# Two transformer blocks on one core: products moved between engines, keys repeated by transfers, and work moved around a loop over heads

## The chip, the cores and the metric

One core of a Trainium2 chip runs the whole program; the time is the device time of one execution in microseconds. TensorE (PE) multiplies, VectorE (DVE), ScalarE (ACT) and GpSimd (POOL) do the element-wise work, and SyncE (SP) issues most transfers between the device's memory and the core. Each engine has one stream of instructions, which it takes in order; an instruction that waits holds up the ones behind it on its engine.

## The reference

512 tokens of width 1024 go through two blocks in float32:

```
first block:  x += rms(mixer(rms(x)));  x += rms(memory attention(rms(x)));  x += rms(swiglu(rms(x)))
second block, two layers:
  q, k, v, z_attn, z_ssm, xbc, dt = split(x @ w_in)
  attn = sliding_window_attention(q, k, v, sinks) * silu(z_attn)      16 heads of 64, 4 key heads
  xbc  = silu(causal_conv4(xbc));  xs, B, C = split(xbc)              12 groups of 128 channels
  y    = chunked_state_space(xs, dt, a, B, C) + xs * d_skip           16 heads of 64, chunks of 128
  ssm  = gated_rmsnorm(y, z_ssm)                                      2 groups of 512 channels
  x    = layer_norm(alpha * x + concat(attn, ssm) @ w_out)
```

The memory attention has 4 heads of 128 over 256 memory rows. Its softmax and that of the windows are over keys on the free axis, with queries on partitions.

## The kernel before

Activations lie transposed, channels on 128 partitions and the 512 tokens on the free axis. Every float32 product is made from three products of rounded halves: a value is split into `hi` (rounded by ACT, L107, L129, L132) and `lo` (the rest, by DVE, L108, L130, L133), and `mm3` (L140 to L152) multiplies hi by hi, hi by lo and lo by hi. A *projection* (`proj`, L185) is one weight tile of 1024 columns against the eight tiles of `h`: 24 matmuls of 512 columns. `weights` (L100) gets such a tile: a transfer of 512 KB on SP into `wraw`, then `whi` on ACT and `wlo` on DVE, with three buffers of each. `held` (L111) splits the weights into activation tiles of 512 columns instead (tags G and R, 34 tiles each), which live as long as they are used.

The order on ACT, DVE, POOL and PE is laid out by a planner that takes, at each moment of its own reckoning, the ready instruction that stands first in the program. SP is exempt (`manual_schedule`, L1375): its transfers stay in the program's order.

Memory (`memory`, L721) works on halves A and B of the tokens: queries of A, logits and softmax of A (L743 to L764), queries of B with the values of A in between, then the output product `out(j, c)` (L791) with four tiles of `w_o_mem`, of which three come through `weights`. `post_norm` (L308) gives each half a chain: a norm over the sum of squares (`rstd`, L200), then eight steps that update x, store it to `xd` (L788) and prepare the next stage's `h` (L263 to L266). The swiglu stage begins with four weight tiles at once (L845, L846) and runs `units_by_k` (L160) over half A, then half B.

Each layer of `hybrid` (L885) makes four gates, the convolutions of B and C (`conv`, L901), convolutions 0 to 4 of xs, and then a loop over eight pairs of heads: `decay(j+1)` (two matmuls L1041, relu and exp on ACT L1045 to L1048, a product L1049, on POOL for the even head), `heads(j)` (16 matmuls L1061, 6 matmuls L1067 and DVE's L1069 to L1071), the gate (L1098) and a sum of squares. In between the loop makes one projection for each of j = 0 to 6: convolutions 5 to 7, then four gates. Iteration 6 norms the first group (`gated_norm(0)`, L1073). After the loop come two key projections, each split by halves of 64 partitions and repeated on the other 64 by POOL (L1114), then the values (96 matmuls of 256 columns, L1127 to L1129), `gated_norm(1)`, and attention:

```
q = queries(0)
for t in range(17):
    j, e_ = divmod(t, 2)
    nxt = scores(t, q) if t < 16 else None
    if t: pts[t - 1] = transposed(prs)
```

`scores` (L1136) makes the logits (L1154, L1155), DVE's bias and maximum (L1160), exp (L1164) and the products with the reciprocal sum (L1169: four parts, two on DVE and two on POOL); `transposed` turns the parts on PE (L1183).

Of the kernel before, what the change touches and what calls it, by code (L numbers as in the profile page):

```python
# [8 lines left out]
F32 = mybir.dt.float32  # L9
F32R = mybir.dt.float32r  # L10
AF = mybir.ActivationFunctionType
ALU = mybir.AluOpType

P = 128
S = 512
# [46 lines left out]
class Kern:  # L62
# [4 lines left out]
    def __init__(self, ctx, tc, aps):  # L67
        self.ctx, self.tc, self.nc, self.a = ctx, tc, tc.nc, aps
        pool = lambda name, **kw: ctx.enter_context(tc.tile_pool(name=name, **kw))
        self.cp = pool("const", bufs=1)  # L70
        self.wp = pool("wts", bufs=3)
        self.rp = pool("acts", bufs=1)
        self.sp = pool("small", bufs=1)
        self.pp = pool("psum", bufs=1, space=bass.MemoryType.PSUM)
        self.dp = pool("scratch", bufs=1, space=bass.MemoryType.DRAM)
        self.n = 0
        self.head = None


    def nm(self, s):  # L80
# [19 lines left out]
    def weights(self, src, n=1024):  # L100

        nc = self.nc
        raw = self.wp.tile([P, 1024], F32, tag="wraw", bufs=3, name=self.nm("wraw"))
        nc.sync.dma_start(raw[:, :n], src)
        hi = self.wp.tile([P, 1024], F32R, tag="whi", bufs=3, name=self.nm("whi"))
        lo = self.wp.tile([P, 1024], F32R, tag="wlo", bufs=3, name=self.nm("wlo"))
        nc.scalar.copy(hi[:, :n], raw[:, :n])  # L107
        nc.vector.tensor_tensor(lo[:, :n], raw[:, :n], hi[:, :n].bitcast(F32), ALU.subtract)  # L108
        return hi, lo

    def held(self, src, tag, n=1024):  # L111
# [612 lines left out]
    def memory(self):  # L724


        nc, a = self.nc, self.a
        h, rs = self.h, self.rs
# [14 lines left out]
        def logits(hd, c):  # L743

            kh, kl = mk[hd]
            qh, ql = q[hd]
            bank = self.ps("lg")
            for i in range(2):
                qq = slice(c.start + i * P, c.start + i * P + P)
                for n, (l, r) in enumerate(((qh, kh), (qh, kl), (ql, kh))):  # L750
                    nc.tensor.matmul(bank[:, 256 * i : 256 * i + 256], l[:, qq], r[:, :256], start=n == 0, stop=n == 2)
            st = self.s("st4", (P, 20), 2)
            mx, nm, sm, rc = (st[:, 2 * i : 2 * i + 2] for i in range(4))
            pr = self.f("R")
            nc.vector.tensor_reduce(mx, bank.rearrange("p (b k) -> p b k", b=2), mybir.AxisListType.X, ALU.max)
            r = rs[:, c.start // P : c.start // P + 2]
            nc.vector.scalar_tensor_tensor(nm, mx, -1.0, r, ALU.mult, ALU.mult)
            parts = [pr[:, 256 * i : 256 * i + 256] for i in range(2)]
            for i, p in enumerate(parts):
                nc.scalar.activation(p, bank[:, 256 * i : 256 * i + 256], AF.Exp, bias=nm[:, i : i + 1], scale=r[:, i : i + 1], accum_out=sm[:, i : i + 1])  # L760
            nc.vector.reciprocal(rc, sm)
            for i, p in enumerate(parts):
                (nc.vector if i else nc.gpsimd).tensor_scalar(p, p, rc[:, i : i + 1], 1.0, ALU.mult, ALU.mult)
            return parts  # L764

        def values(hd, c, prs):
# [18 lines left out]

        def each(k, c, x):
            scale(k, c, x)
            nc.scalar.dma_start(self.xd[k][:, c], x)  # L788

        def out(j, c):  # L790
            o = self.ps()[:, :256]  # L791
# [8 lines left out]
            nc.sync.dma_start(kv[i].bitcast(F32), self.spill[i])  # L800
        wo = [self.held(a["w_o_mem"][0], "G")]
        queries(B, lambda k: values(k // 2, A, pa[k // 2]) if k % 2 else None)
        wo += [self.weights(a["w_o_mem"][1]), self.weights(a["w_o_mem"][2])]
        for j in range(8):
            if j == 4:
                wo.append(self.weights(a["w_o_mem"][3]))
            out(j, A)
            if j < 4:
                pb.append(logits(j, B))
        for j in range(4):  # L810
            values(j, B, pb[j])
            if j == 0:
                self.head = chain(A)
                self.begin()
# [7 lines left out]
    def ffn(self):  # L822
# [19 lines left out]
        full = slice(0, S)  # L842
        hid += self.pairs("R", 2)
        g = [self.f("ht") for _ in range(2)]
        first = [self.weights(z) for z in (a["w_gate"][0], a["w_up"][0], a["w_gate"][1])]  # L845
        first.append(self.held(a["w_up"][1], "R"))  # L846
        for c in self.HALVES:
            for i, pt in enumerate(self.units_by_k(first, h, c)):
                (up if i % 2 else gate)(i // 2, c, g[i // 2][:, c], pt)
# [15 lines left out]

        def src(k, c):
            t = self.s("w256", (P, 256), 9)
            nc.scalar.dma_start(t, self.xd[k][:, c])
            return t

        self.h = self.pairs("G")
# [15 lines left out]
    def hybrid(self, L):  # L887
# [25 lines left out]
        def silu(t, pz):  # L913

            self.tanh(t, pz, scale=0.5)
            nc.vector.scalar_tensor_tensor(t, t, 1.0, pz, ALU.add, ALU.mult)
# [113 lines left out]
            xs.append(conv(j, "G"))  # L1030
        xs.append(conv(4, "G"))
        tokens(0)

        def decay(j):

            ee = self.f("R")
            dfs = []
            for e_ in range(2):
                hd = 2 * j + e_
                pb = self.ps("lg")  # L1040
                nc.tensor.matmul(pb, self.sel[:, hd : hd + 1].broadcast_to([48, P]), ahl, start=True, stop=True)  # L1041
                df = self.f("R")
                for c in range(4):
                    cc = slice(c * P, (c + 1) * P)
                    nc.scalar.activation(df[:, cc], pb[:, cc], AF.Relu, bias=atok[:, c * 16 + hd : c * 16 + hd + 1], scale=-1.0)  # L1045
                rows = slice(64 * e_, 64 * e_ + 64)
                nc.scalar.activation(ee[rows, P:], pb[rows, P:], AF.Exp)
                nc.scalar.activation(df, df, AF.Exp, scale=-1.0)  # L1048
                (nc.vector if e_ else nc.gpsimd).tensor_tensor(df, df, cb[hd // 8], ALU.mult)  # L1049
                dfs.append(df)  # L1050
            return dfs, ee

# [26 lines left out]
                cat[8 + i] = self.pair(t, "R")  # L1079


        cat = [None] * 16
        accs = []
        ws = decay(0)
        for j in range(8):
            g = j // 4
            if j < 3:
                xs.append(conv(5 + j, "G"))
            elif j < 7:
                zs.append(self.f("R"))  # L1090
                silu(zs[-1], self.proj(W[25 + j], h))
            nxt = decay(j + 1) if j < 7 else None
            if j == 3:
                tokens(1)
            heads(j, *ws)
            ws = nxt
            y = xs[j]
            nc.vector.tensor_tensor(y, y, zs[j], ALU.mult)  # L1098
            if j == 6:
                gated_norm(0, accs[0])  # L1100
            if j % 4 == 0:
                accs.append(self.f("acc"))
            self.sumsq(y, accs[-1], j % 4 == 0)


        top, bot = slice(0, 64), slice(64, P)
        kt = []
        for j in range(2):
            pt = self.proj(W[j], h)
            ks = [[self.r("G") for _ in range(2)] for _ in range(2)]  # L1110
            for (kh, kl), r, o in zip(ks, (top, bot), (bot, top)):
                self.split(pt[r], kh[r], kl[r], 0.125)
                for t in (kh, kl):
                    nc.gpsimd.tensor_copy(t[o], t[r].bitcast(F32))  # L1114
            kt.append(ks)
        vs = [self.f("G") for _ in range(2)]
        pv = [self.ps("mm") for _ in range(2)]
        for c in range(2):
            wh, wl = self.weights(W[2 + c])
            for t in range(4):  # L1120
                o = pv[t // 2][:, 256 * (t % 2) : 256 * (t % 2) + 256]
                tt = slice(t * P, (t + 1) * P)
                for kk in range(4):
                    k = 4 * c + kk
                    ws = slice(256 * kk, 256 * kk + 256)
                    st = k == 0 and t % 2 == 0
                    nc.tensor.matmul(o, h[k][0][:, tt], wh[:, ws], start=st, stop=False, skip_group_check=True)  # L1127
                    nc.tensor.matmul(o, h[k][0][:, tt], wl[:, ws], start=False, stop=False, skip_group_check=True)
                    nc.tensor.matmul(o, h[k][1][:, tt], wh[:, ws], start=False, stop=k == 7, skip_group_check=True)  # L1129
        for v, pt in zip(vs, pv):  # L1130
            nc.scalar.copy(v, pt)

        gated_norm(1, accs[1])

        def scores(t, q):
# [30 lines left out]
            nc.vector.tensor_tensor(sm, sm, es, ALU.add)  # L1166
            nc.vector.reciprocal(rc, sm)  # L1167
            for b in range(4):
                (nc.gpsimd if b % 2 else nc.vector).tensor_scalar(prs[b], prs[b], rc[:, b : b + 1], 1.0, ALU.mult, ALU.mult)  # L1169
            return prs  # L1170

        def transposed(prs):
# [34 lines left out]
            return qs  # L1207


        q = queries(0)  # L1210
        gate, pts = {}, {}
        prs = None
        for t in range(17):
# [17 lines left out]
                cat[i] = self.pair(gate[i], "R", 0.5)  # L1231
            prs = nxt

        order = list(range(8, 16)) + list(range(8))
        acc, acc2, rs = self.f("acc"), self.f("acc"), self.f("rs")
        vs = [self.f("G") for _ in range(KD)]
# [186 lines left out]
```

## Time and profile before

| | us |
|---|---|
| median of 3 runs (1672.94 to 1673.29) | 1673.09 |
| profiled execution, its own time | 1672.5 |
| its span, first to last instruction | 1670.7 |
| PE busy, share of the span | 1621.6, 97% |
| DVE, ACT, POOL busy | 1115.1, 838.0, 239.2 |

The span has 24187 instructions, 9046 of them matmuls. A busy PE is not PE at its peak, since ends of matmuls are modelled; the granted clock has two levels, 2.4 GHz (written 1.00) and 1.2 GHz (0.50).

### The profile page before, as it was taken

The numbers are of one execution on the slowest core, as the hardware profiler recorded it, in microseconds if no ns is written. First come the engines' busy times: TensorE is split into PE (matmuls) and PEld (weight loads), VectorE is DVE, ScalarE is ACT, GpSimd is POOL, SyncE is SP. The second block draws the span as 40 slices with busy tenths as digits, with TensorE's granted clock in tenths as the row PEclk, the third lists the DMA queues.
The fourth block names the chain that finished last, engine by engine and source line by source line (L and its number), as shares of the span: only waits on it lengthen the run. The fifth ranks groups of instructions, "written<-read, shape, count | busy, mean of one in ns | idle before, by whom it ended". The sixth has DMA issues, their size and how long they took to land.

```text
span 1670.7 us, 24187 instructions
## 1 busy us (share of the span) xinstructions
PE 1621.6 (97%) x9046; PEld 1362.4 (82%) x9046; DVE 1115.1 (67%) x2199; ACT 838.0 (50%) x1648; POOL 239.2 (14%) x267
## 2 busy tenths in 40 slices
PE   8999999999999999999999999999999999999996
PEld 5778888889888888889988677777998867777786
DVE  6779866548885545523677888765487788866447
ACT  4443255336763233223554776664355477766424
POOL 2010113010200000000000223221230023222121
PEclk9999999999999999999999999999999999999998
DMA  6522322143143233234632122111452211212133
GB/s 223 196 96 76 119 96 76 64 151 119 62 150 104 89 101 101 87 102 129 212 93 89 38 64 89 64 64 56 141 177 82 79 38 57 96 61 65 66 103 112
DMA packets 57719, 166.50 MB, mean 100 GB/s; under 512 B 6673, under 2 KB 15841, under 8 KB 57601
## 3 DMA queue, kind: packets, MB, share of 16 engines
q1 hardware_dynamic: 49216, 155.21, 29.0%
q10 hardware_dynamic: 8384, 9.73, 1.8%
q8 instruction: 71, 1.16, 0.3%
q14 instruction: 48, 0.39, 0.1%
HBM read 158.61 MB, written 8.93 MB: 100 GB/s over the span
## 4 chain that ended last, share of the span: by engine, by line
PE 78%; DVE 11%; ACT 5%; issue 2%; POOL 2%; DMA 1%; SPq 0%; ACTq 0%; DVEq 0%; POOLq 0%
PE psmm L148 21%; PE psmm L152 21%; PE psmm L147 21%; DVE wlo L108 2%; POOL w L1169 2%; PE psmm L175 2%; PE psmm L173 2%; PE psmm L174 2%; ACT w L1164 1%; DVE w L1160 1%; DVE G L130 1%; PE pstr L1061 1%; PE pstr L1183 1%; PE pslg L561 1%; PE pslg L1020 1%
## 5 line engine op out<-in xcount | busy, mean ns | idle before, releaser
L147 PE MATMUL psmm<-G,whi 128*128 128x512 f32 (+1 forms) x1196 | 468.5, 393 | 1.3 <-ACT whi L107 1.3
L148 PE MATMUL psmm<-G,whi 128*128 128x512 f32 (+1 forms) x1196 | 464.3, 389 | 0.0
L108 DVE TENSOR_TENSOR wlo<-wraw,whi 128x1024 fp32r<-128x1024 f32 (+3 forms) x265 | 320.4, 1210 | 184.8 <-ACT whi L107 99.2
L107 ACT CAST whi<-wraw 128x1024 fp32r<-128x1024 f32 (+3 forms) x265 | 270.9, 1025 | 340.3 <-PE psmm L148 291.3
L152 PE MATMUL psmm<-G,wlo 128*128 128x512 f32 (+1 forms) x1196 | 296.3, 388 | 0.0
L148 PEld LDWEIGHTS psmm<-G,whi 128*128 128x128 f32 x1196 | 225.3, 188 | 47.2 <-issue 4.2
L147 PEld LDWEIGHTS psmm<-G,whi 128*128 128x128 f32 x1196 | 225.3, 188 | 47.2 <-issue 2.4
L152 PEld LDWEIGHTS psmm<-G,wlo 128*128 128x128 f32 x1196 | 222.7, 189 | 46.4 <-issue 1.5
L148 PE MATMUL psmm<-R,whi 128*128 128x256 f32 (+1 forms) x732 | 222.7, 326 | 0.0
L147 PE MATMUL psmm<-R,whi 128*128 128x256 f32 (+1 forms) x732 | 222.6, 326 | 0.0
L147 PEld LDWEIGHTS psmm<-R,whi 128*128 128x128 f32 x732 | 139.2, 190 | 11.8 <-issue 0.3
L148 PEld LDWEIGHTS psmm<-R,whi 128*128 128x128 f32 x732 | 139.2, 190 | 11.5
L152 PE MATMUL psmm<-R,wlo 128*128 128x256 f32 (+1 forms) x732 | 138.1, 326 | 0.0
L152 PEld LDWEIGHTS psmm<-R,wlo 128*128 128x128 f32 x732 | 112.8, 190 | 11.5
L198 POOL TENSOR_TENSOR acc<-acc,sq 128x512 f32<-128x512 f32 (+1 forms) x42 | 53.4, 1272 | 454.4 <-ACT sq L197 454.4
L1164 ACT ACTIVATE w<-w,st 128x256 f32<-128x256 f32 (+1 forms) x128 | 60.2, 471 | 33.5 <-DVE st L1162 33.2
L1169 POOL TENSOR_SCALAR w<-w,st 128x256 f32<-128x256 f32 x64 | 46.1, 730 | 134.6 <-DVE st L1167 127.0
L209 ACT ACTIVATE sq<-ht 128x512 f32<-128x512 f32 (+1 forms) x48 | 29.4, 613 | 58.5 <-DVE ht L907 29.3
L1049 POOL TENSOR_TENSOR R<-R,R 128x512 f32<-128x512 f32 x16 | 21.7, 1353 | 228.3 <-ACT R L1048 228.3
L907 DVE SCALAR_TENSOR_TENSOR ht<-psmm,cwh,ht 128x511 f32<-128x511 f32 (+2 forms) x72 | 53.5, 743 | 1.2
L837 DVE TENSOR_TENSOR sq<-psmm,G 128x512 f32<-128x512 f32 (+1 forms) x24 | 15.5, 645 | 57.3 <-PE psmm L152 57.3
L566 POOL TENSOR_TENSOR G<-G,G 128x384 f32<-128x384 f32 (+2 forms) x24 | 28.9, 1217 | 162.1 <-DMA G<-ts 93.4
(348 smaller groups left out, 2701.8 us busy)
## 6 DMA issues: line engine op xcount, KB each, us to landing
wraw<-w_in SPq DMA_DIRECT2D x112, 512.0 KB, 3.4
wraw<-w_out SPq DMA_DIRECT2D x56, 512.0 KB, 3.8
wraw<-w_down SPq DMA_DIRECT2D x24, 512.0 KB, 3.5
wraw<-w_gate SPq DMA_DIRECT2D x22, 512.0 KB, 3.3
wraw<-w_up SPq DMA_DIRECT2D x22, 512.0 KB, 3.3
wraw<-w_down SPq DMA_DIRECT2D x12, 384.0 KB, 3.2
wraw<-w_proj_attn SPq DMA_DIRECT2D x8, 512.0 KB, 3.4
ts<-t SPq DMA_DIRECT2D x4, 640.0 KB, 7.0
```

The lines of the kernel that those rows point to most:

```text
L107: nc.scalar.copy(hi[:, :n], raw[:, :n])
L108: nc.vector.tensor_tensor(lo[:, :n], raw[:, :n], hi[:, :n].bitcast(F32), ALU.subtract)
L147: nc.tensor.matmul(out, whi[:, c], xh, start=start and k == 0, stop=False)
L148: nc.tensor.matmul(out, whi[:, c], xl, start=False, stop=False)
L152: nc.tensor.matmul(out, wlo[:, c], xh, start=False, stop=stop and k == n - 1)
L173: nc.tensor.matmul(o, whi[:, cc], xh[:, c], start=k == 0 and i % 2 == 0, stop=False, skip_group_check=True)
L174: nc.tensor.matmul(o, whi[:, cc], xl[:, c], start=False, stop=False, skip_group_check=True)
L175: nc.tensor.matmul(o, wlo[:, cc], xh[:, c], start=False, stop=k == n - 1, skip_group_check=True)
L198: (eng or nc.gpsimd).tensor_tensor(acc, acc, t, ALU.add)
L907: nc.vector.scalar_tensor_tensor(y[:, s:], pt[:, : S - s], cw(3 - s), y[:, s:], ALU.mult, ALU.add)
L1164: nc.scalar.activation(prs[b], prs[b], AF.Exp, bias=nm[:, b : b + 1], accum_out=sm[:, b : b + 1])
L1169: (nc.gpsimd if b % 2 else nc.vector).tensor_scalar(prs[b], prs[b], rc[:, b : b + 1], 1.0, ALU.mult, ALU.mult)
```

## The change

Seven edits. (1) All softmax products of memory and of the windows go to DVE. (2) Between the start of attention and its end, `lo` of a weight tile is made in two pieces of 512 columns. (3) The stores to and loads from `xd` go from ACT's queue to SP's. (4) Memory's output weights 1 to 3 are held in R tiles, all loaded before `out`, and the first three weight tiles of the swiglu stage are asked for before the values of half B. (5) Convolutions 5 and 6 stand ahead of the loop. (6) In the loop, the even head's relu goes to DVE (as a minimum with the sign turned) and its product from POOL to DVE. (7) The loop's projections are now convolution 7, four gates, the values (j = 5) and the two keys (j = 6 and 7); the keys are repeated by four transfers on SP each.

```diff
+        self.piece = 2 * S
...
-        nc.vector.tensor_tensor(lo[:, :n], raw[:, :n], hi[:, :n].bitcast(F32), ALU.subtract)
+        for o in range(0, n, self.piece):
+            c = slice(o, min(o + self.piece, n))
+            nc.vector.tensor_tensor(lo[:, c], raw[:, c], hi[:, c].bitcast(F32), ALU.subtract)
...
-                (nc.vector if i else nc.gpsimd).tensor_scalar(p, p, rc[:, i : i + 1], 1.0, ALU.mult, ALU.mult)
+                nc.vector.tensor_scalar(p, p, rc[:, i : i + 1], 1.0, ALU.mult, ALU.mult)
...
-            nc.scalar.dma_start(self.xd[k][:, c], x)
+            nc.sync.dma_start(self.xd[k][:, c], x)
...
-        wo += [self.weights(a["w_o_mem"][1]), self.weights(a["w_o_mem"][2])]
+        wo += [self.held(a["w_o_mem"][j], "R") for j in (1, 2, 3)]
         for j in range(8):
-            if j == 4:
-                wo.append(self.weights(a["w_o_mem"][3]))
             out(j, A)
             if j < 4:
                 pb.append(logits(j, B))
+        self.ahead = [self.weights(z) for z in (a["w_gate"][0], a["w_up"][0], a["w_gate"][1])]
...
-        first = [self.weights(z) for z in (a["w_gate"][0], a["w_up"][0], a["w_gate"][1])]
-        first.append(self.held(a["w_up"][1], "R"))
+        first = self.ahead + [self.held(a["w_up"][1], "R")]
...
-            nc.scalar.dma_start(t, self.xd[k][:, c])
+            nc.sync.dma_start(t, self.xd[k][:, c])
...
         tokens(0)
+        for j in range(5, 7):
+            xs.append(conv(j, "G"))
...
+                    if e_:
+                        nc.scalar.activation(df[:, cc], pb[:, cc], AF.Relu, bias=at, scale=-1.0)
+                    else:
+                        nc.vector.tensor_scalar(df[:, cc], pb[:, cc], at, 0.0, ALU.subtract, ALU.min)
...
-                (nc.vector if e_ else nc.gpsimd).tensor_tensor(df, df, cb[hd // 8], ALU.mult)
+                nc.vector.tensor_tensor(df, df, cb[hd // 8], ALU.mult)
...
+        def keys(j):
+            pt = self.proj(W[j], h)
+            ks = [[self.r("G") for _ in range(2)] for _ in range(2)]
+            for (kh, kl), r, o in zip(ks, (top, bot), (bot, top)):
+                self.split(pt[r], kh[r], kl[r], 0.125)
+                for t in (kh, kl):
+                    nc.sync.dma_start(t[o].bitcast(F32), t[r].bitcast(F32))
+            return ks
...
-            if j < 3:
-                xs.append(conv(5 + j, "G"))
-            elif j < 7:
+            if j == 0:
+                xs.append(conv(7, "G"))
+            elif j < 5:
                 zs.append(self.f("R"))
-                silu(zs[-1], self.proj(W[25 + j], h))
+                silu(zs[-1], self.proj(W[27 + j], h))
+            elif j == 5:
+                vs = token_values()
+            else:
+                kt.append(keys(j - 6))
...
-                for t in (kh, kl):
-                    nc.gpsimd.tensor_copy(t[o], t[r].bitcast(F32))
...
-                (nc.gpsimd if b % 2 else nc.vector).tensor_scalar(prs[b], prs[b], rc[:, b : b + 1], 1.0, ALU.mult, ALU.mult)
+                nc.vector.tensor_scalar(prs[b], prs[b], rc[:, b : b + 1], 1.0, ALU.mult, ALU.mult)
...
+        self.piece = S
         q = queries(0)
```

`token_values` is the loop that made the values before, unchanged.

## Rows read from the trace of the kernel before

**Rows 1.** The page's first part: busy time, share of the span and instructions of each engine.
```profile
PE 1621.6 (97%) x9046; PEld 1362.4 (82%) x9046; DVE 1115.1 (67%) x2199; ACT 838.0 (50%) x1648; POOL 239.2 (14%) x267
```

**Rows 2.** The waits of PE: who waited for whom, total us, times, longest.
```profile
PE pstr L1183 <- POOL w L1169: 5.7, 14, 0.6
PE pslg L1154 <- DVE G L130: 5.0, 2, 2.5
PE pstr L1061 <- POOL R L1049: 2.1, 2, 1.3
...
PE pstr L204 <- DVE G L1069: 0.7, 2, 0.5
```

**Rows 3.** Stretches of the span: length, then busy us (and instructions) of PE, PEld, DVE, ACT, POOL, the granted clock of PE, DMA share, GB/s. The first two are a wait in memory and the time after it, the last two the same ahead of attention in the first layer.
```profile
462.90:466.60 3.70, 0.28 (x3) 0.09 (x2) 3.33 (x9) 3.70 (x12) 0.00 (x0) 1.00 0.30 106
466.60:473.40 6.80, 6.46 (x25) 5.66 (x26) 5.34 (x8) 5.12 (x9) 0.00 (x0) 0.50 0.53 154
...
1022.50:1025.10 2.60, 0.08 (x2) 0.03 (x1) 2.54 (x5) 1.10 (x4) 0.00 (x0) 1.00 0.17 25
1026.40:1029.80 3.40, 3.40 (x10) 2.63 (x9) 3.34 (x11) 2.18 (x3) 0.00 (x0) 0.51 0.02 5
```

**Rows 4.** One softmax of attention in order of time (start us, us, engine, line): DVE's two products and the `lo` of weights after them, POOL's two products, and the last transposes on PE.
```profile
1088.31 0.78 DVE L1169 TENSOR_SCALAR w<-w,st 128x128 f32<-128x128 f32 x2
1089.01 1.21 DVE L108 TENSOR_TENSOR wlo<-wraw,whi 128x1024 fp32r<-128x1024 f32 x1
...
1088.44 2.04 POOL L1169 TENSOR_SCALAR w<-w,st 128x256 f32<-128x256 f32 x2 [5.34 <-DVE st L1167]
...
1090.53 0.44 PE L1183 MATMUL pstr<-ident,w 128*128 128x128 f32 x2 [0.40 <-POOL w L1169]
```

**Rows 5.** Groups by line with shapes kept apart (busy us, mean ns): products of a tile with a column on DVE, a read of a PSUM tile by DVE, the odd and even heads' product, and ACT's `whi`.
```profile
L453 DVE TENSOR_SCALAR G<-G,st 128x256 f32<-128x256 f32 x8 | 2.8, 347 | 0.1
L453 DVE TENSOR_SCALAR G<-G,st 128x128 f32<-128x128 f32 x8 | 2.2, 281 | 0.0
L217 DVE TENSOR_SCALAR acc<-pstr 128x256 f32<-128x256 f32 x11 | 4.6, 421 | 6.0 <-PE pstr L204 5.8
L1049 DVE TENSOR_TENSOR R<-R,R 128x512 f32<-128x512 f32 x16 | 10.9, 683 | 0.4 <-ACT R L1048 0.4
...
L1049 POOL TENSOR_TENSOR R<-R,R 128x512 f32<-128x512 f32 x16 | 21.7, 1353 | 228.3 <-ACT R L1048 228.3
...
L107 ACT CAST whi<-wraw 128x1024 fp32r<-128x1024 f32 x243 | 254.6, 1050 | 283.5 <-PE psmm L148 248.1 <-PE psmm L174 14.0 <-issue 9.3
```

**Rows 6.** SP in order of time in the mixer's end and memory (a merged row has the time from its first to its last transfer), and the page's DMA issues (count, KB, median us from issue to landing).
```profile
384.21 5.60 SPq L735 DMA_DIRECT2D G<-spill  x4
392.12 1.75 SPq L800 DMA_DIRECT2D G<-spill  x4
393.99 0.35 SPq L115 DMA_DIRECT2D wraw<-w_o_mem  x1
...
wraw<-w_in SPq DMA_DIRECT2D x112, 512.0 KB, 3.4
```

**Rows 7.** Splits by halves of 64 partitions, in order of time: a key's (first `hi` on ACT, last `lo` on DVE), then a query's (`hi` on ACT, `lo` on DVE, twice).
```profile
998.19 0.57 ACT L132 ACTIVATE G<-psmm 64x512 fp32r<-64x512 f32 x1
...
1003.96 0.69 DVE L133 SCALAR_TENSOR_TENSOR G<-psmm,G 64x512 fp32r<-64x512 f32 x1
...
1030.65 0.58 ACT L129 CAST G<-psmm 64x512 fp32r<-64x512 f32 x1 [1.24 <-PE psmm L152]
1031.98 0.58 ACT L129 CAST G<-psmm 64x512 fp32r<-64x512 f32 x1 [0.75 <-DVE G L130]
...
1031.26 0.68 DVE L130 TENSOR_TENSOR G<-psmm,G 64x512 fp32r<-64x512 f32 x1 [0.57 <-ACT G L129]
...
1032.83 0.69 DVE L130 TENSOR_TENSOR G<-psmm,G 64x512 fp32r<-64x512 f32 x1
```

**Rows 8.** PE in order of time: the matmuls of one pair of heads, the decay of the next, and the matmul of a norm.
```profile
965.57 1.09 PE L1061 MATMUL pstr<-R,G 128*64 128x128 f32 x16
966.60 0.94 PE L1067 MATMUL pstr<-R,R 128*128 128x128 f32 x6
967.46 0.72 PE L1041 MATMUL pslg<-ahl,selr 48*128 48x512 f32 x2
...
987.27 1.12 PE L204 MATMUL pstr<-acc,ones 128*128 128x512 f32 x2 [0.47 <-DVE G L1069]
```

**Rows 9.** The start of the swiglu stage in order of time: ACT's `whi` of its first three weight tiles and the last square of half B, PE's norm of the stage's input and the norm that begins half B's chain, and the last `lo` of the stage's input.
```profile
466.14 2.97 ACT L107 CAST whi<-wraw 128x1024 fp32r<-128x1024 f32 x3
...
470.28 0.36 ACT L197 ACTIVATE sq<-psmm 128x256 f32<-128x256 f32 x1
...
466.61 1.19 PE L204 MATMUL pstr<-acc,ones 128*128 128x256 f32 x2 [3.43 <-DVE acc L198]
...
473.50 0.59 PE L204 MATMUL pstr<-acc,ones 128*128 128x256 f32 x2
...
489.74 0.47 DVE L265 SCALAR_TENSOR_TENSOR G<-G,vecs,G 128x256 fp32r<-128x256 f32 x1
```

**Rows 10.** The sum over the stretch from 956 to 1026 us, the loop over heads and what follows it up to attention (columns as in rows 3), and one stretch of attention.
```profile
sum 70.00, PE 66.24 PEld 52.79 DVE 58.70 ACT 50.53 POOL 21.25; mean PE 9.46 PEld 7.54 DVE 8.39 ACT 7.22 POOL 3.04
...
1040.00:1120.00 80.00, 77.90 (x449) 63.10 (x448) 54.81 (x160) 49.62 (x132) 17.83 (x30) 1.00 0.20 66
```

More of the change, by code (lines that the diff above doesn't have):

```diff
@@ L1044, in decay @@
                     cc = slice(c * P, (c + 1) * P)
-                    nc.scalar.activation(df[:, cc], pb[:, cc], AF.Relu, bias=atok[:, c * 16 + hd : c * 16 + hd + 1], scale=-1.0)
+                    at = atok[:, c * 16 + hd : c * 16 + hd + 1]
+                    if e_:
+                        nc.scalar.activation(df[:, cc], pb[:, cc], AF.Relu, bias=at, scale=-1.0)
+                    else:
+                        nc.vector.tensor_scalar(df[:, cc], pb[:, cc], at, 0.0, ALU.subtract, ALU.min)
                 rows = slice(64 * e_, 64 * e_ + 64)
                 nc.scalar.activation(ee[rows, P:], pb[rows, P:], AF.Exp)
-                nc.scalar.activation(df, df, AF.Exp, scale=-1.0)
-                (nc.vector if e_ else nc.gpsimd).tensor_tensor(df, df, cb[hd // 8], ALU.mult)
+                nc.scalar.activation(df, df, AF.Exp, scale=-1.0 if e_ else 1.0)
+                nc.vector.tensor_tensor(df, df, cb[hd // 8], ALU.mult)
                 dfs.append(df)
@@ L1079, in gated_norm, with token_values @@
                 cat[8 + i] = self.pair(t, "R")
+        top, bot = slice(0, 64), slice(64, P)
+        kt = []
+        def keys(j):
[6 more added lines that the diff above has]
+            return ks
+        def token_values():
+            vs = [self.f("G") for _ in range(2)]
+            pv = [self.ps("mm") for _ in range(2)]
+            for c in range(2):
+                wh, wl = self.weights(W[2 + c])
+                for t in range(4):
+                    o = pv[t // 2][:, 256 * (t % 2) : 256 * (t % 2) + 256]
+                    tt = slice(t * P, (t + 1) * P)
+                    for kk in range(4):
+                        k = 4 * c + kk
+                        ws = slice(256 * kk, 256 * kk + 256)
+                        st = k == 0 and t % 2 == 0
+                        nc.tensor.matmul(o, h[k][0][:, tt], wh[:, ws], start=st, stop=False, skip_group_check=True)
+                        nc.tensor.matmul(o, h[k][0][:, tt], wl[:, ws], start=False, stop=False, skip_group_check=True)
+                        nc.tensor.matmul(o, h[k][1][:, tt], wh[:, ws], start=False, stop=k == 7, skip_group_check=True)
+            for v, pt in zip(vs, pv):
+                nc.scalar.copy(v, pt)
+            return vs
         cat = [None] * 16
@@ L1103, in hybrid @@
             self.sumsq(y, accs[-1], j % 4 == 0)
[L1106 to L1112, printed above, removed]
-                for t in (kh, kl):
-                    nc.gpsimd.tensor_copy(t[o], t[r].bitcast(F32))
[L1115 to L1131, printed above, removed]
         gated_norm(1, accs[1])
@@ L1232, in hybrid @@
             prs = nxt
+        self.piece = 2 * S
         order = list(range(8, 16)) + list(range(8))
```

## The prediction

> **What bounds the kernel now.** The totals come first [rows 1]: PE is busy for 1621.6 of 1670.7 us, so that all its idle time is 49.1 us, and no engine beside it is near that. The change adds and takes no matmul. It can therefore only give PE idle time back, or make some, or change the clock that follows an idle. So the second view is the list of PE's waits [rows 2], the third the stretches around the longest of them [rows 3], where the clock stands at its half level right after an idle of over 2.5 us: a 3.4 us wait in memory is followed by 6.8 us at 0.50, and a 2.5 us wait ahead of attention by 3.4 us at 0.51. Then come the rows in order of time for each edit's place [rows 4, 6 to 9], and the engines' load in the loop and in attention [rows 10].
>
> **What is removed.**
> (a) Softmax products. POOL takes 2.04 us for two, DVE 0.78 for two, and PE's transposes stand 0.40 behind POOL's second [rows 4]; over both layers 14 such waits cost 5.7 [rows 2]. On DVE all four end some 1.6 us after the first begins (2 x 0.78) if nothing of another kind comes between, earlier than POOL's two. What could come between is a `lo` of weights of 1.21 [rows 4], and edit 2 halves it, so DVE can lag by some 0.6. DVE is busy for 54.8 of 80 us in attention [rows 10]; 64 products move, at 281 ns, the row of a 128x128 product [rows 5], or 0.39: 18 to 25 us over two attention stages of over 200 us altogether, where DVE has a third of its time free. That is hidden, and 5.7 goes. If DVE lags by 0.6 at each of the 14 places, 8.4 us come back and 2.7 is lost; I take the 5.7, since no row shows DVE late here.
> (b) Ahead of attention PE waits 2.5 us in each layer for the query's `lo` [rows 2], and 3.4 us at 0.51 behind it cost 3.4 x 0.49 = 1.7 [rows 3]; I take 1.6 for each of two layers, as the second was not read as closely: 5.0 + 3.2 = 8.2. The two-piece `lo` lets the query's split in sooner; the values and keys are out of the way. It goes only if something covers it; the part on the keys below says what does.
> (c) In the loop PE waits 2.1 for the even head's product on POOL, and 0.7 for DVE ahead of a norm [rows 2]. On DVE the product takes 0.68 in place of 1.35 [rows 5]: 2.1 + 0.7 = 2.8 goes.
> (d) Memory to swiglu. ACT makes `whi` of the first three swiglu tiles only at 466.14, because the output weights hold the three buffers; the last square of half B stands behind them at 470.28 [rows 9]. With held output weights these tiles are ready earlier and PE has matmuls for the 3.43 us wait, and so for the 6.8 us at half clock, worth 3.4: 6.8. If only the weights come earlier but half B's chain, whose norm is at 473.50 and whose last `lo` at 489.74 [rows 9], does not, PE meets it later, and I put the lower end at 1.5, less than half of the wait. I take 6.8, since the three casts of 2.97 us are what the square waits behind.
> Sum: 5.7 + 8.2 + 2.8 + 6.8 = 23.5.
>
> **What is added without a cost that I can see.** Convolutions 5 and 6 are moved whole; their loads keep their order among w_in's. They take DVE's work out of the loop, where DVE is busy for 58.7 of 70 us [rows 10]. Against that the even head's relu costs DVE four operations a pair, in no row before: a 128x128 product takes 281 ns, a read of PSUM twice as wide 421 [rows 5]; at 0.3 four are 1.2, with the product 0.68 that is 1.9 a pair and 15 in eight pairs, with the rest 74 of 70 us, less the two convolutions that leave the loop, whose `lo` of 1.21 alone make 2.4. DVE is thus close to full; bounds 0 to +5 a layer, 0 taken, because PE has matmuls of projections to take in between. SP's added transfers of x (edit 3) cost SP about 0.35 each as the issue of [rows 6] does; the load of one swiglu tile behind A's stores may be late, 0 to +2, 0 taken. Held output weights need twelve R tiles more than none; their loads follow the values' on SP at 394 [rows 6], 70 us ahead of their use.
>
> **What is added with a cost: the keys' transfers.** SP takes its transfers in the program's order: the first load of w_o_mem is issued at 393.99, behind four loads from the spill that hold SP for 5.60 and 1.75 us [rows 6]. In the changed loop a key's projection is followed on SP by its four transfers, each of which waits for a split, and only behind them comes the next weight tile: key 1's behind key 0's, and the first query's behind key 1's. Before, the loads ran up to three tiles ahead, and POOL did the copies. The wait of PE for the next tile then is, from the end of a key's projection:
> split by halves, `hi` on ACT, `lo` on DVE, twice: 1030.65 to 1033.52 in the shortest row, 2.9; key 0's, with ACT and DVE in other work, 998.19 to 1004.65, 6.5 [rows 7];
> one issue, 0.35, and the landing of 512 KB, 3.4 [rows 6]; `whi` on ACT, 1.05 [rows 5].
> Sum 2.9 + 0.35 + 3.4 + 1.05 = 7.7, and two of them in each layer, 15.4.
> PE has for these gaps the pairs of heads that are left, each 1.09 + 0.94 = 2.0, decays at 0.72, and norms of 1.12 for two matmuls, 0.56 for one [rows 8]: three pairs, two decays and one norm's matmul give 6.0 + 1.4 + 0.6 = 8.0 when the heads run one pair late; two pairs, one decay and two of the norm's give 5.8. With 8.0, 7.4 is idle; and as idles of 2.5 and 3.4 us were followed by 3.4 and 6.8 us at half clock [rows 3], I add 1.7 for one such stretch in a layer: 9.1, in two layers 18.2. Bounds: if everything is hidden, 0; with the longer split on both keys, 11.3 x 2 - 5.8 + 3.4 = 20.2 a layer.
> The Trainium skill speaks against this price ("DMA: Bandwidth & Descriptors", section "Issuing engines are not separate DMA queues"): which engine issues a transfer decides only where its issue time is paid, and all share the same DMA engines. By that alone the transfers would cost SP four issues a key and PE nothing, the first rival; the row above of loads behind waiting spill loads says that on SP the wait itself is paid too.
>
> **Sum.** On the profiled execution 1672.5 - 23.5 + 18.2 = 1667.2; that execution lies 0.6 below the median of 1673.09, so 1667.8, and I write 1667.5.
>
> **Rivals.**
> A, gains only. The split ends early or the planner of the order keeps enough of heads' work back that the loads' lateness is covered: 1673.1 - 23.5 = 1649.6. For it: PE's instructions stand in an order that reckons with late tiles. Against: 8.0 us of spare matmuls for 15.4 of waiting.
> B, slower. The place is the same, the queue of SP behind a key's split, with the split at 5.3, between the two rows [rows 7], because DVE is near full (58.7 of 70 [rows 10]) and the even heads' relu comes to it: 10.1 x 2 - 5.8 + 3.4 = 17.8 a layer, 35.6 - 23.5 = +12.1, 1685.2. It decides from an added 11.8 us a layer on.
> C, no change. The transfers cost their 18.2, but memory gives back 1.5 only, or DVE, with all products, takes (a)'s gain: 1667.5 + 5.3 = 1672.8.
>
> **How the numbers follow.** Forecast 0.45, from 1660 to 1675 by the cover of 5.8 to 8.0 and one or two stretches at half clock; A 0.20; B 0.25; C 0.10. Within 0.2%, 3.3 us, a measurement can't tell from no change. Faster: three quarters of the forecast and all of A, 0.54; slower: B and a little of the forecast, 0.27; the rest, 0.19. The range reaches from A's 1649 to 1685, where B stands.
>
> **What will show it.** Right: in the changed trace SP stands at the keys' transfers, and PE waits for `whi` of key 1 and of the first query, 3 to 4 us each in both layers, with half clock behind; the waits of [rows 2] for POOL are gone, and memory's end has no stretch at 0.50. Wrong: no wait of PE at these two tiles (A), or idles above 6 us there (B); a new wait of PE for DVE's products in attention or for the even heads' in the loop would say that DVE has become the bound, which I priced at nothing.

## The result, and the profile after

The changed kernel takes 1691.3 us (median of 4 runs, 1690.5 to 1692.3) against 1673.0 for the kernel before in the same runs: a ratio of 1.011, with an interval of 1.0093 to 1.0128. It is slower by 18 us, outside the predicted range.

The waits of PE in the changed kernel (who waited for whom, total us, times, longest), three that were not there before, or were small, and one that has shrunk:

```profile
PE psmm L150 <- ACT whi L108: 15.0, 6, 7.9
PE pstr L207 <- POOL acc L201: 7.2, 2, 5.0
...
PE psmm L780 <- ACT ht L132: 2.3, 2, 2.1
...
PE pstr L1198 <- DVE w L1184: 1.4, 5, 0.4
```

L108 is the `whi` of a weight tile; at the same line of `mm3` such waits were 1.3 us before. L1198 turns the windows' products on PE: it waited 5.7 us for POOL's [rows 2] and a little for DVE's,

```profile
PE pstr L1183 <- DVE w L1169: 0.6, 2, 0.3
```

and waits 1.4 now. So one of the things that were to go has gone, and something larger has come.

SP in order of time at the end of the first layer's loop (L1099 is a key's transfer, L105 the load of a weight tile):

```profile
1003.38 3.44 SPq L1099 DMA_DIRECT2D G<-G  x4
1006.87 0.58 SPq L105 DMA_DIRECT2D wraw<-w_in  x1
1018.58 4.10 SPq L1099 DMA_DIRECT2D G<-G  x4
1022.73 15.97 SPq L105 DMA_DIRECT2D wraw<-w_in  x6
```

Each key's four transfers hold SP for 3.4 and 4.1 us, and the load behind them leaves only then. PE at the end of each key's projection, and at the first matmul on the tile that came late:

```profile
1012.19 0.50 PE L150 MATMUL psmm<-G,whi 128*128 128x512 f32 x1 [1.25 <-ACT whi L108]
...
1022.95 2.08 PE L207 MATMUL pstr<-acc,ones 128*128 128x512 f32 x2 [5.02 <-POOL acc L201]
1028.12 0.80 PE L150 MATMUL psmm<-G,whi 128*128 128x512 f32 x1 [3.10 <-ACT whi L108]
```

Key 1's tile finds PE with two pairs of heads to do, and PE waits for it only 1.25 us; the rest of its idle there lies between the matmuls of the heads, which have no projection beside them. The first query's finds one norm (L207) and nothing else: 5.02 and 3.10 us of waiting. The same stretches by windows (length, then busy us and instructions of PE, PEld, DVE, ACT, POOL, granted clock, DMA share, GB/s), layer one and then, in a fence of its own, layer two:

```profile
1002.60:1012.20 9.60, 6.16 (x50) 3.98 (x49) 8.82 (x17) 7.83 (x15) 0.92 (x1) 1.00 0.41 112
...
1017.90:1028.10 10.20, 2.10 (x3) 0.50 (x2) 4.92 (x9) 5.22 (x9) 1.67 (x2) 0.67 0.62 195
1028.10:1031.70 3.60, 3.58 (x8) 2.81 (x9) 3.60 (x6) 2.38 (x3) 0.00 (x0) 0.50 0.25 77
```
```profile
1419.90:1429.10 9.20, 6.12 (x49) 3.97 (x48) 8.47 (x16) 7.74 (x15) 0.90 (x1) 1.00 0.42 116
...
1434.80:1446.10 11.30, 1.29 (x4) 0.33 (x3) 10.43 (x15) 7.01 (x11) 2.32 (x2) 0.64 0.53 161
1446.10:1451.50 5.40, 5.40 (x13) 4.24 (x14) 5.40 (x10) 3.03 (x4) 0.00 (x0) 0.50 0.43 150
```

Idle time of PE is length less busy: 3.4 and 8.1 us in the first layer, 3.1 and 10.0 in the second. Behind the longer hole the clock stands at its half level: 3.60 us worth 1.8 at full clock and 1.0 in the norm itself (2.08 us in place of 1.12 [rows 8]) in the first layer, 5.40 us worth 2.7 in the second. Together 14.3 and 15.8 us.

Memory, which was to give 6.8 us, gave nothing. ACT, DVE and PE in order of time, where half B's values begin:

```profile
445.95 3.01 ACT L108 CAST whi<-wraw 128x1024 fp32r<-128x1024 f32 x3
448.78 0.67 ACT L132 CAST ht<-pstr 128x512 fp32r<-128x512 f32 x1
...
447.11 3.50 DVE L111 TENSOR_TENSOR wlo<-wraw,whi 128x1024 fp32r<-128x1024 f32 x3 [0.51 <-ACT whi L108]
...
446.75 0.67 PE L207 MATMUL pstr<-acc,ones 128*128 128x256 f32 x2 [1.70 <-DVE acc L201]
449.50 0.58 PE L780 MATMUL psmm<-ht,G 128*128 128x256 f32 x1 [2.09 <-ACT ht L132]
451.26 0.58 PE L781 MATMUL psmm<-sq,G 128*128 128x256 f32 x1 [1.17 <-DVE sq L133]
```

The window around these waits (columns as above):

```profile
444.40:454.80 10.40, 5.44 (x23) 4.02 (x21) 7.09 (x12) 7.42 (x16) 0.00 (x0) 0.67 0.00 0
```

The three casts that stood at 466.14 [rows 9] stand at 445.95 now, and what they hold up is the split of the turned probabilities (`ht`, `sq`), for which PE waits 2.09 and 1.17 us. In 10.4 us PE is busy for 5.4, at a mean clock of 0.67: the hole and the half clock of [rows 3], twenty microseconds earlier.

### The profile page after: what moved, and what is told of

It is laid out like the page before. It is cut to its first block, busy times and chain, and to the rows that moved or that the text cites. A ratio compares the mean times of both kernels' runs of the same rounds, so it can differ in the third digit from the quotient of the medians.

```text
span 1688.9 us, 24140 instructions
## 1 busy us (share of the span) xinstructions
PE 1626.1 (96%) x9046; PEld 1366.0 (81%) x9046; DVE 1136.5 (67%) x2386; ACT 809.8 (48%) x1579; POOL 153.8 (9%) x163
## 4 chain that ended last, share of the span: by engine, by line
PE 81%; DVE 11%; ACT 4%; issue 2%; DMA 1%; POOL 0%; DVEq 0%; SPq 0%; ACTq 0%; POOLq 0%
PE psmm L150 21%; PE psmm L151 21%; PE psmm L155 21%; DVE wlo L111 1%; PE pstr L1198 1%; ACT w L1179 1%; PE psmm L1213 1%; PE psmm L178 1%; PE psmm L176 1%; PE psmm L177 1%; DVE w L1175 1%; PE pstr L1068 1%; PE psmm L687 1%; PE pslg L1169 1%; PE pslg L564 1%
## 5 line engine op out<-in xcount | busy, mean ns | idle before, releaser
L108 ACT CAST whi<-wraw 128x1024 fp32r<-128x1024 f32 (+3 forms) x262 | 267.5, 1024 | 352.7 <-PE psmm L151 308.9
L150 PEld LDWEIGHTS psmm<-G,whi 128*128 128x128 f32 x1196 | 226.5, 189 | 65.0 <-ACT whi L108 18.2
L151 PE MATMUL psmm<-R,whi 128*128 128x256 f32 (+1 forms) x684 | 210.5, 329 | 0.0
L150 PE MATMUL psmm<-R,whi 128*128 128x256 f32 (+1 forms) x684 | 210.4, 329 | 0.0
L150 PEld LDWEIGHTS psmm<-R,whi 128*128 128x128 f32 x684 | 130.0, 190 | 11.8 <-issue 0.3
L151 PEld LDWEIGHTS psmm<-R,whi 128*128 128x128 f32 x684 | 130.0, 190 | 11.5
L155 PE MATMUL psmm<-R,wlo 128*128 128x256 f32 (+1 forms) x684 | 130.3, 329 | 0.0
L155 PEld LDWEIGHTS psmm<-R,wlo 128*128 128x128 f32 x684 | 106.2, 190 | 11.5
L200 ACT ACTIVATE sq<-G 128x256 f32<-128x256 f32 (+1 forms) x76 | 35.2, 463 | 34.8 <-DVE G L1270 19.2
L1175 DVE CUSTOM_DVE_ANT_0 w<-pslg,w,sinks 128x256 f32<-128x256 f32 (+1 forms) x128 | 51.1, 446 | 0.3
L1157 POOL TENSOR_SCALAR w<-dist 128x256 f32<-128x256 f32 x32 | 23.7, 740 | 298.9 <-PE pstr L1198 219.1
```

Of the source, the lines that this page charges most:

```text
L150: nc.tensor.matmul(out, whi[:, c], xh, start=start and k == 0, stop=False)
L151: nc.tensor.matmul(out, whi[:, c], xl, start=False, stop=False)
L155: nc.tensor.matmul(out, wlo[:, c], xh, start=False, stop=stop and k == n - 1)
L200: self.last_sq = nc.scalar.activation(t, src, AF.Square)
L1157: nc.gpsimd.tensor_scalar(al, self.dist, -SLOPES[head], 1.0, ALU.mult, ALU.mult)
L1175: nc.vector.tensor_tensor_reduce(pr, pt, al[:, 256 - n :], 1.0, sink, ALU.add, ALU.max, mx[:, b : b + 1])
```

## The experiments

The theory: the key transfers' place on SP costs about 28 us, the removed waits gave about 10. The rivals: the keys' new place in the loop or a full DVE costs the time, or the transfers themselves do.

**The next tile asked for ahead of the key's transfers.**

```diff
-            pt = self.proj(W[j], h)
+            if j == 0:
+                tile.append(self.weights(W[0]))
+            else:
+                self.piece = S
+            pt = self.proj(None, h, w=tile[j])
+            tile.append(self.weights(W[1] if j == 0 else W[16]))
...
-            pt = self.proj(W[16 + j], h)
+            pt = self.proj(W[16 + j], h, w=None if j else tile[2])
```

> The changed kernel, with the weight tile that follows a key asked for ahead of that key's split and transfers (key 1's tile with key 0's projection, the first query's with key 1's), so that SP issues these two loads before it waits. Theory (loads held behind waiting transfers): the two holes of PE in each layer, 3.4 and 8 us of idle in the first and the half clock behind them, go; about 13 us a layer, 26 in all: 1665 us, faster than the changed kernel by 1.3 to 1.7%. Rival (the splits are late because DVE is full, and PE waits for them wherever the loads stand): under 8 us back, 1683 or more, with the waits moved to the first scores.

Measured 1673.1 us, ratio to the kernel before 1.0007 (0.9998 to 1.0016). Two thirds of the loss come back, not all. SP in order of time, and the wait of PE at the first scores:

```profile
1003.68 3.44 SPq L1104 DMA_DIRECT2D G<-G  x4
1007.17 1.30 SPq L105 DMA_DIRECT2D wraw<-w_in  x1
1013.01 8.89 SPq L1104 DMA_DIRECT2D G<-G  x4
...
1022.73 0.33 PE L1174 MATMUL pslg<-G,G 128*128 128x128 f32 x1 [3.40 <-DVE G L133]
1026.11 2.08 PE L207 MATMUL pstr<-acc,ones 128*128 128x512 f32 x2 [1.95 <-POOL acc L201]
```

The two tiles come in time, but key 1's transfers hold SP for 8.89 us, and now the tile behind the first query is late: no projection is there to cover the query's split, and PE waits for its `lo` at the first scores, 3.40 us, as it did before the change (2.5), with half clock behind (0.69 on the mean from 1019.2 to 1030.3 us). The hole has moved on by one tile. That is the theory's mechanism, and an expected size that forgot it.

**The keys repeated by POOL's copies, in the loop.**

```diff
-                    nc.sync.dma_start(t[o].bitcast(F32), t[r].bitcast(F32))
+                    nc.gpsimd.tensor_copy(t[o], t[r].bitcast(F32))
```

> The changed kernel with the keys repeated by POOL's copies again, in the loop where the projections now are; SP has no transfer that waits for a split. Theory (SP's order is the cost): as with the tiles asked for early, about 1665 us; POOL is idle there, so its copies need not delay the first scores. Rival (moving the keys into the loop is what costs): 1683 or more.

Measured 1665.8 us, ratio 0.9959 (0.9945 to 0.9973), as the theory has it. The keys' place in the loop is not the cost.

**The same transfers, issued by POOL.**

```diff
-                    nc.sync.dma_start(t[o].bitcast(F32), t[r].bitcast(F32))
+                    nc.gpsimd.dma_start(t[o].bitcast(F32), t[r].bitcast(F32))
```

> The changed kernel with the keys' four transfers issued by POOL instead of SP; they are the same transfers, with the same waits, but no weight load stands behind them. Theory (SP's order is the cost): as with POOL's copies, 1664 to 1668 us, and no wait of PE for the whi of key 1 or of the first query. Rival (the transfers themselves are slow or crowd the loads): 1675 or more.

Measured 1662.9 us, ratio 0.9945 (0.9931 to 0.996). One word of the code is worth some 28 us: from 1.1% above the kernel before to 0.55% below it. POOL in order of time:

```profile
1003.26 0.73 POOL L1099 DMA_DIRECT2D G<-G  x1 [1.66 <-DVE R L1052]
1004.35 1.04 POOL L1099 DMA_DIRECT2D G<-G  x2 [0.36 <-issue]
1005.98 0.52 POOL L1099 DMA_DIRECT2D G<-G  x1 [0.59 <-PE psmm L150]
```

The first layer's transfers (count, KB, median us to landing), from SP in the changed kernel and from POOL in this one, and by windows the stretch of PE in which the two holes lay:

```profile
G<-G SPq DMA_DIRECT2D x8, 128.0 KB, 2.3
```
```profile
G<-G POOLq DMA_DIRECT2D x8, 128.0 KB, 2.7
```
```profile
1002.00:1022.00 20.00, 20.00 (x114) 15.75 (x113) 18.92 (x33) 14.12 (x26) 6.13 (x10) 1.00 0.38 103
```

POOL waits for the same splits, 1003 to 1006.5 us, and no weight load stands behind it. The transfers land no sooner than from SP, and PE is busy for the whole of the 20 us.

**Memory's edits alone, in the kernel before** (output weights held, first tiles early, xd's transfers on SP: the diff of the change, edits 3 and 4).

> The kernel before with the edits on memory alone (output weights 1 to 3 held, the swiglu stage's first three tiles asked for before the values of half B, xd's transfers on SP). Theory (the three casts of 3 us on ACT and 3.5 us on DVE only move the hole of PE from the stage's end to half B's values): 1672 to 1675 us, no change. Rival (the edit is worth the wait that it removes, and the changed kernel loses it elsewhere): 1666 us.

Measured 1673.6 us, ratio 1.0009 (0.9999 to 1.0018). They give nothing, also without the rest of the change.

**The products alone, in the kernel before** (edit 1).

> The kernel before with the softmax products of memory and of the windows on DVE alone. Theory (the 14 waits of PE for POOL, 5.7 us, go and DVE has room): 1667 to 1668 us. Rival (DVE takes the wait over): 1672 us or more.

Measured 1670.4 us, ratio 0.9988 (0.9978 to 0.9997). Between theory and rival: 2.0 us, not 5.7. The wait that is left, then DVE and PE in order of time in one softmax:

```profile
PE pstr L1183 <- DVE w L1169: 1.6, 9, 0.2
```
```profile
1105.80 1.07 DVE L1169 TENSOR_SCALAR w<-w,st 128x128 f32<-128x128 f32 x4
1106.79 1.22 DVE L108 TENSOR_TENSOR wlo<-wraw,whi 128x1024 fp32r<-128x1024 f32 x1
...
1106.23 1.14 PE L1183 MATMUL pstr<-ident,w 128*128 128x128 f32 x7 [0.15 <-DVE w L1169]
```

All four products take DVE 1.07 us, where POOL took 2.04 for two [rows 4]; PE comes to them before they are done. The waits for both engines, 5.7 and 0.6 us, became 1.6 for DVE. In the two profiles PE's idle fell by as much as the list promised, from 49.1 to 44.1 us (span less busy), but its busy time rose from 1621.6 to 1625.3. Some 1.6 us of that is a stretch at half clock near 45 us, ahead of all these edits, that the kernel before has not (from 44 to 50 us a mean clock of 0.72 against 1.00); why the rest did not turn up in the time is left open.

**The lo of weights in one piece again** (with POOL's copies of the keys).

```diff
-        self.piece = S
         q = queries(0)
```

> The changed kernel with POOL's copies of the keys (1665.8 us) and with the lo of weights in one piece again during attention. Theory (products on DVE alone still wait behind a lo of 1.2 us, as the run with the products alone showed with 1.6 us of waits left; the two pieces take that away and let the query's split in): 1668 to 1671 us. Rival (the pieces do nothing): 1665.8.

Measured 1666.7 us, ratio 0.9963 (0.995 to 0.9976), against 0.9959 with the pieces: 0.9 us between the medians, inside the intervals. The rival.

**Swiglu's first tiles asked for after half B's values** (with POOL's copies).

```diff
-        self.ahead = [self.weights(z) for z in (a["w_gate"][0], a["w_up"][0], a["w_gate"][1])]
         for j in range(4):
             values(j, B, pb[j])
...
+        self.ahead = [self.weights(z) for z in (a["w_gate"][0], a["w_up"][0], a["w_gate"][1])]
         for j in range(8):
             self.pump(1)
             out(j, B)
```

> The changed kernel with POOL's copies of the keys and with the swiglu stage's first three tiles asked for after the values of half B, ahead of the output product of half B (11 us of matmuls). Theory (their casts, 3.0 us on ACT and 3.5 on DVE, stood ahead of the splits that PE waited for, 5 us and a half clock of 6.8 us): they fall beside matmuls now, and 5 to 8 us go: 1658 to 1661 us. Rival (the casts then stand ahead of half B's squares and chain, and the hole comes back at the stage's start): 1664 to 1666.

Measured 1664.5 us, ratio 0.9951 (0.9936 to 0.9966): 1.3 us between the medians, with intervals that overlap. The hole in the values has shrunk, and another has come at the second part of the stage; SP and PE in order of time:

```profile
477.72 11.16 SPq L791 DMA_DIRECT2D xd<-G  x8
488.97 0.38 SPq L105 DMA_DIRECT2D wraw<-w_gate  x1
...
494.06 0.77 PE L150 MATMUL psmm<-G,whi 128*128 128x512 f32 x1 [2.02 <-ACT whi L108]
```

It is the keys' pattern once more: the stores of half B's x to `xd`, moved from ACT's queue to SP's by edit 3, wait for their x one by one and hold SP for 11.16 us; the next weight tile leaves behind them. In the changed kernel the same stores hold SP for 10.24 and 11.16 us, and yet PE is busy for 24.1 of the 25 us from 472 to 497: a held queue costs only where the tile behind it has no cover.

**The even head's relu on ACT and its product on POOL again** (with POOL's copies).

```diff
-                    if e_:
+                    if True:
                         nc.scalar.activation(df[:, cc], pb[:, cc], AF.Relu, bias=at, scale=-1.0)
...
-                nc.scalar.activation(df, df, AF.Exp, scale=-1.0 if e_ else 1.0)
-                nc.vector.tensor_tensor(df, df, cb[hd // 8], ALU.mult)
+                nc.scalar.activation(df, df, AF.Exp, scale=-1.0)
+                (nc.vector if e_ else nc.gpsimd).tensor_tensor(df, df, cb[hd // 8], ALU.mult)
```

> The changed kernel with POOL's copies of the keys and with the even head's relu on ACT and its product on POOL again. Theory (the two waits for POOL's product come back, some 1 to 2 us a layer): 1667 to 1670 us. Rival (DVE is near full in the loop and has been the bound there): 1663 or less.

Measured 1665.7 us, ratio 0.9963 (0.9949 to 0.9977), against 1665.8 with the edit: no difference. Neither theory's 2 us nor the rival's full DVE.

**Late tiles and xd's transfers on POOL's queue** (with the keys' transfers there too).

```diff
-            nc.sync.dma_start(self.xd[k][:, c], x)
+            nc.gpsimd.dma_start(self.xd[k][:, c], x)
...
-            nc.sync.dma_start(t, self.xd[k][:, c])
+            nc.gpsimd.dma_start(t, self.xd[k][:, c])
```

> The changed kernel with the keys' transfers on POOL's queue (1662.9 us), the swiglu stage's first tiles asked for after half B's values, and xd's stores and loads on POOL's queue too. Theory (xd's stores wait for their x on SP and hold the next swiglu tiles, 11 us behind half B's chain in the run before, as the keys' transfers did; and the early casts were the wait in half B's values): both holes of memory shrink and 4 to 6 us go: 1657 to 1659 us. Rival (the holes of memory are the chain of norms itself and only move): 1661 to 1663.

Measured 1662.3 us, ratio 0.9938 (0.9924 to 0.9951), against 0.9945: the rival. The loads are in time, but PE waits for a split of the stage's held weights in place of the cast (the list of waits, then the window around it):

```profile
PE psmm L178 <- DVE R L133: 2.1, 1, 2.1
```
```profile
465.80:472.80 7.00, 4.87 (x26) 4.48 (x26) 4.18 (x11) 3.81 (x11) 2.27 (x5) 0.76 0.53 184
```

**Memory as before** (with the keys' transfers on POOL's queue; edits 3 and 4 undone).

> The changed kernel with the keys' transfers on POOL's queue and memory as it was in the kernel before (output weights through the weights' buffers, the first tiles asked for at the stage's start, xd's transfers on ACT's queue; the products stay on DVE). Theory (the edits on memory are worth nothing together, as the run with them alone showed): 1661.5 to 1663.5 us. Rival (with DVE's products in memory they give their 5 us): 1667.

Measured 1661.6 us, ratio 0.9934 (0.9921 to 0.9946): no different from 0.9945 with the edits, which says again that edits 3 and 4 are worth nothing in either surrounding.

**The loop's new order alone, in the kernel before** (edits 5 and 7, transfers on POOL's queue).

> The kernel before with the new order of the loop alone (convolutions 5 and 6 ahead of it, values and keys in it) and the keys' transfers on POOL's queue; products, lo, memory and decay as before. Theory (the wait of 2.5 us ahead of attention and the half clock behind it, 8.2 us over both layers, are what the order removes, by itself): 1663.5 to 1666 us. Rival (the order needs the products off POOL or the lo in two pieces to give anything): 1669 or more.

Measured 1666.5 us, ratio 0.9961 (0.9949 to 0.9974): 6.8 us less, close to the theory's range. The order gives this by itself, but not as the theory says. At the first scores PE still waits, for other engines (the list of waits, then the windows around them in both layers):

```profile
PE pslg L1171 <- ACT sq L200: 3.4, 2, 1.7
PE pstr L207 <- POOL acc L201: 2.8, 2, 1.4
```
```profile
1018.00:1036.00 18.00, 14.51 (x60) 11.11 (x59) 15.53 (x35) 10.03 (x21) 4.78 (x5) 0.81 0.10 31
1426.00:1444.00 18.00, 14.41 (x64) 11.24 (x64) 16.56 (x36) 10.55 (x22) 4.77 (x5) 0.91 0.08 30
```

These 6.2 us stand where 5.0 stood for the query's `lo` [rows 2], and a mean clock of 0.81 and 0.91 over 18 us is some 6.8 and 3.2 us at half level. What has gone from the list is the wait for POOL's product (2.1) and the one for DVE ahead of a norm (0.7). PE's idle over the span is 47.6 us against 49.1, its busy time 1617.1 against 1621.6; where most of the 6.8 us comes from is left open.

**The change without the edits on memory and on the decay** (products on DVE, lo in pieces, the loop's order, the keys' transfers on POOL's queue).

> The changed kernel with the keys' transfers on POOL's queue, memory as before, and the even head's relu on ACT and its product on POOL as before; of the change this leaves the products on DVE, the two pieces of lo and the order of the loop. Theory (memory's edits and the decay's give nothing): 1660.5 to 1663 us, the same as with the decay's edit. Rival (the decay's edit is needed once the loads are in time): 1665.

Measured 1661.0 us, ratio 0.993 (0.9917 to 0.9944). It beats both kernels, the one before by 12 us and the changed one by 30. Against 0.9934 with the decay's edit it is no different.

## Why the prediction was wrong

The mechanism of the cost and its place were in the prediction, its size was not, and three of the four gains set against it were too large. In the predicted sum, 23.5 us of gains met 18.2 of cost; the runs have about 10 against 28. Of the 23.8 us between forecast and result, the larger part, some 14, is thus gains that did not come, and some 10 the cost.

**The keys' transfers (18.2 predicted, about 28 measured).** That loads wait on SP behind the transfers is shown twice over: with the same transfers on another queue the time falls by 28 us, and with the loads ahead of the transfers the wait moves to the first load that is still behind them. The failed term is the stretch from a key's projection to the next tile, 7.7 us, above all the split in it at 2.9, the shortest row [rows 7]. In the changed kernel key 1's split and the next tile's `whi` read, in the first layer and in the second (ACT's first `hi`, in the first layer a step of a norm on DVE, DVE's last `lo`, then `whi`):

```profile
1017.96 0.59 ACT L135 ACTIVATE G<-psmm 64x512 fp32r<-64x512 f32 x1 [1.75 <-PE psmm L155]
...
1017.63 1.40 DVE L1085 SCALAR_TENSOR_TENSOR ht<-G,vecs,rs 128x512 f32<-128x512 f32 x2
...
1021.46 0.69 DVE L136 SCALAR_TENSOR_TENSOR G<-psmm,G 64x512 fp32r<-64x512 f32 x1
...
1027.04 1.03 ACT L108 CAST whi<-wraw 128x1024 fp32r<-128x1024 f32 x1
...
1435.18 0.57 ACT L135 ACTIVATE G<-psmm 64x512 fp32r<-64x512 f32 x1
...
1439.92 0.69 DVE L136 SCALAR_TENSOR_TENSOR G<-psmm,G 64x512 fp32r<-64x512 f32 x1
...
1444.97 1.04 ACT L108 CAST whi<-wraw 128x1024 fp32r<-128x1024 f32 x1
```

The splits take 4.2 and 5.4 us, since `gated_norm(0)` (L1085 and its splits) has its steps on the same two engines between the halves; key 0's take 3.5 in each layer. From the last `lo` to the start of `whi` it is another 4.9 and 4.4 us, where one issue and one landing, 3.75, were reckoned; SP issues the load 0.6 us behind the split. From a key's projection to the first matmul on the next tile it was 9.6 and 10.2 us in the first layer, 9.2 and 11.3 in the second, where 7.7 was reckoned: 4.4 and 5.1 us more in a layer, of which the splits make 1.9 and 3.1. The cover was about as predicted: PE had 6.16 + 2.10 and 6.12 + 1.29 us of work in the holes, against 8.0. The clock's share was 2.8 and 2.7 us a layer instead of 1.7, as the second hole is longer than any of [rows 3]. Rival B named this wait with the split at 5.3 and the price of 17.8 a layer; measured by the windows it was 14.3 and 15.8, above the 11.8 from which B decides. The sign that the prediction gave for B, idles above 6 us at these tiles, is there with 8.1 and 10.0.

The rule that the prediction set against this price, in the Trainium skill ("DMA: Bandwidth & Descriptors", section "Issuing engines are not separate DMA queues"), holds for the transfers: they landed in 2.3 us from SP and 2.7 from POOL. For the program's time it did not decide, because here SP pays not only the issue but the wait for the data, as its rows of 3.44 to 8.89 us show. The same page of the Trainium skill says in its section "Anatomy of one DMA — SWDGE (gpsimd) path" that a wait on a semaphore happens on the issuing sequencer, ahead of dispatch; these rows agree.

**Memory (6.8 predicted, none measured).** The step that failed is "PE has matmuls for the 3.43 us wait". It took the three casts as something that gets out of the way if it is done earlier. They take 3.0 us of ACT and 3.5 of DVE wherever they are put, both engines stand in the chain of half B's values, and PE's wait moved to them with its half clock. The other place for them that was tried, behind half B's values, moved it again, in both runs that have it.

**Products (5.7 predicted, 2.0 alone).** The list of waits names the wait for POOL, not what comes next: PE arrives before DVE's four products too, and 1.6 us of waits remain. That PE's idle fell by 5.0 us and the time by 2.0 shows the step that failed: idle that goes was put down as time that goes, and PE's busy time rose.

**Decay (2.8 predicted, none measured)**: with the edit and without it the times are 1665.8 and 1665.7. The list of the run without it has no wait of PE for POOL's product, nor has that of the loop's order alone, where the product is on POOL too: the order had taken these 2.1 us away, and the sum put them down to the edit.

**The wait ahead of attention (8.2 predicted).** The loop's order alone gives 6.8. The size is right, and by luck: in that run PE waits 6.2 us at the first scores, not 5.0, with half clock behind, so that the wait has changed its engines and not gone. The text also leant on the two-piece `lo`, whose 0.9 us is inside the intervals. The fear that DVE would be the bound (C, and part of B) was not borne out: 1136.5 us of DVE's time in the changed kernel, and the same 1136.3 in the one with the transfers on POOL's queue, which is 28 us faster.

The gains together: 6.8 from the order, 2.0 from the products, 0.9, if it is one, from the pieces: 9.7, and the changed kernel with the transfers on POOL's queue is 9.4 us faster than the kernel before (1662.9 against 1672.3).

## What to carry to other kernels

A transfer that waits for the result of an engine does not belong in the queue that feeds the weights; put it where nothing stands behind it, and judge a move between queues by what is queued next, not by the transfer. When a chain's duration in its new place is needed, take it from rows with the same neighbours, not from the shortest: here 2.9 us became 4.2 and 5.4 because a norm ran on the same engines. And an early request moves the casts too: ask which chain they will stand in before counting a wait as gone, and whether another edit of the same change already takes it away.

## What was not expected of the hardware

The half clock behind a hole can cost as much as a short hole itself, and its length does not follow from the hole alone. After 2.5 us it lasted 3.4, after 3.4 us 6.8 [rows 3], and in the changed kernel from inside the longer hole to its end and 3.6 or 5.4 us beyond, so that a hole of 8 to 10 us cost 2.7 to 2.8 us more. But with the loop's order alone the same two waits, 1.7 and 1.4 us, were followed by some 6.8 us at half level in the first layer and 3.2 in the second. A short stretch of the same kind comes without any change near it: 3.4 us at half level at 45 us in the run with POOL's copies, at full clock in the one with the transfers on POOL's queue, though this part of the kernel is the same; seven of the fourteen profiles have it, the changed kernel's among them, and the one of the kernel before has not:

```profile
45.10:48.50 3.40, 3.06 (x14) 3.06 (x15) 3.38 (x7) 1.75 (x5) 0.00 (x0) 0.50 0.81 269
```
```profile
44.00:49.00 5.00, 3.84 (x30) 3.64 (x31) 4.81 (x8) 3.06 (x6) 0.00 (x0) 1.00 1.06 337
```

It is worth about 1.6 us, as much as some of the edits tried here; differences of that size between single profiles are not read as an edit's effect.
